# A two-layer hybrid encoder in split float32r products: operand start addresses moved to multiples of 256 bytes, and the head norm's weights applied at the transpose

## The chip, the cores and the metric

The kernel runs on one NeuronCore of one Trainium2 chip. The metric is the device time of one execution in microseconds, the median of several. Before the change that median is 2259.04 us, over three runs from 2258.91 to 2259.23 us.

## What is computed

An input of 256 tokens by 2048 features goes through two layers in float32. Layer 0 has one input projection whose columns feed a bidirectional matrix memory (four heads) and a bidirectional gated recurrence, and one output projection. Layer 1 has windowed attention with 16 heads. Each is followed by a gated feed-forward block, and every block begins with an RMS norm. The part of the reference that the change touches is the end of layer 0's mixer:

```python
hm = bidirectional_mlstm(qh, kh, vh, gates)
hm = hm * lax.rsqrt(jnp.mean(jnp.square(hm), axis=-1, keepdims=True) + RMS_EPS)
hm = jnp.transpose(hm, (0, 2, 1, 3)).reshape(B, S, MLSTM_WIDTH) * head_g.astype(jnp.float32)
y_a = hm * jax.nn.sigmoid(o.astype(jnp.float32))
...
y = jnp.concatenate([y_a, y_b], axis=-1).astype(h.dtype)
return y @ w_out
```

Here `head_g` has one weight for each of the 1024 features of `hm`.

## The kernel before

**Products.** Nearly all the work is the product of 256 tokens with about 400 MB of weights. To keep float32 accuracy each operand is split in two float32r parts, a high one (the value rounded to float32r) and a low one (what is left). The weights arrive through SP's DMA queue as tiles `raw` of 1 MB (four buffers). For each half of such a tile ScalarE casts the high part (`wh`, L204) and VectorE subtracts it to get the low part (`wl`, L205), three steps ahead of TensorE.

A matrix instruction has a **held** operand (128 columns, loaded into the array by a weight load that the trace shows on its own engine, PEld) and a **streamed** operand. There are two shapes of step:

- *Wide* steps (L294 and L295) hold 128 columns of weights and stream the activations. L294 holds the high weights and streams both parts of 256 tokens, 512 columns; L295 holds the low weights and streams the high part, 256 columns. All products whose outputs lie on partitions have this shape.
- *Narrow* steps (L272, L273, L274) hold 128 tokens of one part of the activations and stream 512 columns of weights: high by high, high by low, low by high.

Both parts together are 3712 pairs of wide and 3648 narrow instructions. The remaining matrix instructions are small: float32 ones (transposes at L141, the recurrence's gates at L454, the memory's scores at L681) and the attention's float32r ones (L861 to L863).

**Order.** The schedule is written out by hand. `emit_step` records the split of a later step, the products of this step, and then one stage of each background task; evacuations are generators that advance by one `yield` for each step. So the order of instructions on each engine is fixed when the program is built, and does not depend on times.

**Where tiles lie.** A pool allocates its tiles one behind the other in every partition, at byte addresses that follow from the sizes of all tiles allocated ahead of them. Tiles in pool `const` come first, in the order of their allocation (L130 to L138 and small ones later), then `raw`, `wh`, `wl`, 2 KB work tiles (`ev`), eight 8 KB slots (`slot`, of `SLOT` = 2064 floats) that hold activations such as `hT`, `ya`, `yb`, `oT`, `v`, five 4 KB tiles (`m4`, 1040 floats), and small ones. Start addresses in a partition, taken modulo 256, of the tiles that matrix instructions read:

```
tile                          before             after
cst (identity, triangles)     224                0
ehr                           224                0
ones                          32                 0
xT (activations, all wide)    96                 0
wh, wl (every buffer)         32                 0
ev tiles                      32                 0
8 KB slots 0..7               32 96 160 224 ...  0
4 KB tiles 0..4               32 96 160 224 32   0
```

The parts of these tiles that the products take begin at multiples of 512 bytes in them, so the offset of a tile is that of its operands. (In `v`, where a head is 1032 bytes, and for a few operands of 4 columns, this does not hold, before or after.) All starts before are odd multiples of 32 bytes.

**The head norm.** `o_chunk` (L780) makes the output gate: ScalarE writes tanh into an `ev` tile (L789), VectorE adds 1 and multiplies with `hgh`, a tile of 128 by 1024 that holds half of `head_g` on every partition (L794). GpSimd's queue loads it by a broadcast DMA (L999), VectorE halves it (L1002). `ml_out` (L744) multiplies the heads with their norm factors and this gate (L759), transposes the result on TensorE (L771), and splits the transpose into float32r parts (`ya`): a cast on ScalarE (L772) and a subtraction on VectorE (L773), each over two feature blocks at a time.

## Time and profile before

| What | Value |
|---|---|
| median of 3 runs | 2259.04 us |
| span of the profiled execution, first to last instruction | 2256.9 us |
| difference of the two (what lies around the span) | 2.1 us |
| TensorE busy with matrix instructions | 2240.3 us |
| TensorE weight loads | 1903.8 us |
| VectorE busy | 1391.3 us |
| ScalarE busy | 1097.7 us |
| GpSimd busy | 23.8 us |
| read from HBM | 414.09 MB, 184 GB/s over the span |

The busy time of an engine is the time in which at least one of its instructions runs. Matrix instructions overlap: the next starts while the one ahead is still on its way through the array. So a row of a matrix instruction gives a duration that is longer than the step from its start to the start of the next, and it is the step that adds up to the time.

### The profile page before, as it was taken

How to read it: one execution, taken by the hardware profiler on the slowest of the kernel's cores; microseconds unless marked ns; L12 is line 12 of the kernel's file. 1: busy time of each engine (PE TensorE's matmuls, PEld its weight loads, DVE VectorE, ACT ScalarE, POOL GpSimd, SP SyncE). 2: the span in 40 equal slices, each digit the busy share in tenths (PEclk: the TensorE clock that was granted, in tenths of full speed). 3: DMA queues.
4: the chain of work that ended last, by engine and by line, in shares of the span. 5: the costliest groups of instructions: out<-in, count | busy, mean ns of one | idle time of the engine just before them, and what ended most of it. 6: DMA issues, size and time to landing. Idle time of an engine off the chain costs nothing.

```text
span 2256.9 us, 29286 instructions
## 1 busy us (share of the span) xinstructions
PE 2240.3 (99%) x11660; PEld 1903.8 (84%) x11660; DVE 1391.3 (62%) x1960; ACT 1097.7 (49%) x1603; POOL 23.8 (1%) x42
## 2 busy tenths in 40 slices
PE   9999999999999999999999999999999999999998
PEld 7878888888888888888888888888888888888886
DVE  6867856666654466665566676556666544666654
ACT  5667545444443344444454554454444433444443
POOL 1000000000000000000000000000000000000000
PEclk9999999999999999999999999999999999999999
DMA  7534655555555555555555555445555555555553
GB/s 289 182 122 151 221 171 187 187 187 186 187 186 189 184 187 187 187 193 182 191 190 176 186 183 175 168 171 185 185 187 187 204 187 202 191 189 189 192 196 112
DMA packets 61354, 418.09 MB, mean 185 GB/s; under 512 B 6972, under 2 KB 7628, under 8 KB 12448
## 3 DMA queue, kind: packets, MB, share of 16 engines
q1 hardware_dynamic: 58176, 406.35, 52.1%
q0 software_dynamic: 2608, 9.26, 1.2%
q8 instruction: 91, 1.49, 0.3%
q10 hardware_dynamic: 432, 0.60, 0.1%
q14 instruction: 47, 0.39, 0.0%
HBM read 414.09 MB, written 2.10 MB: 184 GB/s over the span
## 4 chain that ended last, share of the span: by engine, by line
PE 95%; DVE 2%; ACT 1%; issue 1%; DMA 0%; SPq 0%; POOL 0%; POOLq 0%; DVEq 0%; ACTq 0%
PE acc L294 37%; PE acc L295 19%; PE acc L272 12%; PE acc L274 12%; PE acc L273 12%; DVE wl L205 1%; PE rgp L454 1%; ACT wh L204 1%; PE nT L141 0%; DVE xc L421 0%; DMA raw<-in_w_v 0%; PE apT L141 0%; PE num L724 0%; PE asc L862 0%; PE apo L861 0%
## 5 line engine op out<-in xcount | busy, mean ns | idle before, releaser
L205 DVE TENSOR_TENSOR wl<-raw,wh 128x1024 fp32r<-128x1024 f32 (+1 forms) x770 | 932.8, 1221 | 727.2 <-ACT wh L204 698.7
L294 PE MATMUL acc<-xT,wh 128*128 128x512 f32 x3712 | 1314.8, 396 | 0.4 <-ACT v L662 0.4
L204 ACT CAST wh<-raw 128x1024 fp32r<-128x1024 f32 (+1 forms) x770 | 802.0, 1044 | 568.3 <-PE acc L274 324.1
L295 PE MATMUL acc<-xT,wl 128*128 128x256 f32 x3712 | 1045.1, 282 | 0.0
L294 PEld LDWEIGHTS acc<-xT,wh 128*128 128x128 f32 x3712 | 697.8, 188 | 165.5 <-ACT v L662 0.6
L295 PEld LDWEIGHTS acc<-xT,wl 128*128 128x128 f32 x3712 | 696.8, 188 | 1.1 <-DVE wl L205 0.3
L272 PE MATMUL acc<-wh,hT 128*128 128x512 f32 x704 | 276.9, 393 | 0.0
L274 PE MATMUL acc<-wh,hT 128*128 128x512 f32 x704 | 275.9, 392 | 0.0
L273 PE MATMUL acc<-wl,hT 128*128 128x512 f32 x704 | 275.7, 392 | 0.0
L274 PEld LDWEIGHTS acc<-wh,hT 128*128 128x128 f32 x704 | 132.2, 188 | 29.9
L273 PEld LDWEIGHTS acc<-wl,hT 128*128 128x128 f32 x704 | 132.4, 188 | 29.0
L272 PEld LDWEIGHTS acc<-wh,hT 128*128 128x128 f32 x704 | 132.3, 188 | 28.8
L313 ACT CAST hT<-up 128x256 fp32r<-128x256 f32 x88 | 35.8, 406 | 198.7 <-DVE up L951 198.7
L934 ACT ACTIVATE up<-up 128x256 f32<-128x256 f32 x88 | 36.8, 418 | 157.8 <-DVE up L933 157.8
L272 PE MATMUL acc<-wh,xT 128*128 128x512 f32 x256 | 104.1, 407 | 0.5 <-ACT wh L204 0.5
L273 PE MATMUL acc<-wl,xT 128*128 128x512 f32 x256 | 101.3, 396 | 1.0 <-DVE wl L205 1.0
L274 PE MATMUL acc<-wh,xT 128*128 128x512 f32 x256 | 101.1, 395 | 0.0
L319 DVE TENSOR_TENSOR up<-acc,up 128x256 f32<-128x256 f32 x176 | 73.5, 418 | 1.5 <-ACT up L318 1.5
L318 ACT COPY up<-acc 128x256 f32<-128x256 f32 x176 | 64.2, 365 | 0.0
L314 DVE TENSOR_TENSOR hT<-up,hT 128x256 fp32r<-128x256 f32 x88 | 37.4, 426 | 41.6 <-ACT hT L313 41.6
L272 PEld LDWEIGHTS acc<-wh,xT 128*128 128x128 f32 x256 | 48.1, 188 | 12.5 <-ACT wh L204 1.5
L273 PEld LDWEIGHTS acc<-wl,xT 128*128 128x128 f32 x256 | 48.1, 188 | 11.8 <-DVE wl L205 1.6
(228 smaller groups left out, 1371.3 us busy)
## 6 DMA issues: line engine op xcount, KB each, us to landing
raw<-in_w SPq DMA_DIRECT2D x264, 1024.0 KB, 4.8
raw<-in_w_aqk SPq DMA_DIRECT2D x32, 1024.0 KB, 4.9
raw<-in_w_out SPq DMA_DIRECT2D x16, 1024.0 KB, 4.8
raw<-in_w_av SPq DMA_DIRECT2D x16, 1024.0 KB, 4.8
raw<-in_w_o SPq DMA_DIRECT2D x16, 1024.0 KB, 4.8
raw<-in_w_xr SPq DMA_DIRECT2D x8, 1024.0 KB, 8.6
raw<-in_w_qk SPq DMA_DIRECT2D x8, 1024.0 KB, 4.9
raw<-in_w_og SPq DMA_DIRECT2D x8, 1024.0 KB, 4.8
```

The source lines that it names most:

```text
L204: A.copy(hi[:, k], raw[:, k])
L205: V.tensor_tensor(lo[:, k], raw[:, k], hi[:, k].bitcast(F32), op=ALU.subtract)
L272: PE.matmul(acc, xh, hi[:, j, :], start=f, stop=False)
L273: PE.matmul(acc, xh, lo[:, j, :], start=False, stop=False)
L274: PE.matmul(acc, xl, hi[:, j, :], start=False, stop=e)
L294: PE.matmul(acc, wh[:, j, :], x2.rearrange("p a b -> p (a b)"), start=f, stop=False)
L295: PE.matmul(acc[:, :S], wl[:, j, :], x2[:, 0, :], start=False, stop=e)
L313: A.copy(dst[:, 0, :], src)
L314: V.tensor_tensor(dst[:, 1, :], src, dst[:, 0, :].bitcast(F32), op=ALU.subtract)
L318: A.copy(dst, acc[:, S:])
L319: V.tensor_tensor(dst, acc[:, :S], dst, op=ALU.add)
L934: A.activation(t, t, AF.Silu)
```

## The change

It does two things. Sizes and the order of allocation are changed so that the tiles of the products begin at multiples of 256 bytes: two tiles of 64 bytes go to the front, `cpk` is padded to 192 floats, a slot has 2112 floats in place of 2064, a 4 KB tile 1088 in place of 1040. And `hgh` shrinks from 1024 floats on every partition to 8: the weights lie by feature in `cpk` (columns 152 to 159), and are multiplied in where the transposed result is split, where a feature is a partition. The gate is then tanh + 1 alone, written in place. The DMA at L999 and the wait for step 16 go. Comments and docstrings are dropped as well, which moves line numbers.

```diff
-C_BA, C_BX, C_LAM = 104, 120, 136
-C_N = 152
+C_BA, C_BX, C_LAM, C_HG = 104, 120, 136, 152
+C_N = 160
...
-SLOT = 2064
+SLOT = 2112
...
-        t = m4p.tile([P, 1040], dt, tag="m4", name=name)
+        t = m4p.tile([P, 1088], dt, tag="m4", name=name)
...
-    cpk = const.tile([P, C_N], F32, name="cpk")
+    gbias = const.tile([P, 16], F32, name="gbias")
+    half = const.tile([P, 16], F32, name="half")
+    cpk = const.tile([P, 192], F32, name="cpk")[:, :C_N]
     cst = const.tile([P, 3, P], F32, name="cst")
     ehr = const.tile([MH, MH, P], F32R, name="ehr")
-    gbias = const.tile([P, 16], F32, name="gbias")
     ones = const.tile([P, P], F32, name="ones")
-    half = const.tile([P, 16], F32, name="half")
-    hgh = const.tile([P, 1024], F32, name="hgh")
     xT = const.tile([P, KB, 2, S], F32R, name="xT")
+    hgh = const.tile([P, 16], F32, name="hgh")[:, :RB]
...
-            A.copy(yt[:, 2 * p:2 * p + 2, 0, :], ps)
-            V.tensor_tensor(
-                yt[:, 2 * p:2 * p + 2, 1, :], ps, yt[:, 2 * p:2 * p + 2, 0, :].bitcast(F32), op=ALU.subtract
-            )
             for k in range(2):
+                kb = 2 * p + k
+                g = hgh[:, 4 * c + kb:4 * c + kb + 1]
+                A.mul(yt[:, kb, 0, :], ps[:, k, :], g)
+                V.scalar_tensor_tensor(
+                    yt[:, kb, 1, :], ps[:, k, :], g, yt[:, kb, 0, :].bitcast(F32), op0=ALU.mult, op1=ALU.subtract
+                )
                 flags.add(f"y{4 * c + 2 * p + k}")
...
-            es = []
+            go = ml["go"][:, :, c * CW:(c + 1) * CW]
             for t in range(2):
-                e = ev("oe")
-                A.activation(e, ch.acc[t], AF.Tanh, scale=ml["ro"][:, t:t + 1])
-                es.append(e)
+                A.activation(go[:, t, :], ch.acc[t], AF.Tanh, scale=ml["ro"][:, t:t + 1])
             ch.acc = None
             yield
-            for t in range(2):
-                V.scalar_tensor_tensor(
-                    ml["go"][:, t, c * CW:(c + 1) * CW], es[t], 1.0, hgh[:, c * CW:(c + 1) * CW],
-                    op0=ALU.add, op1=ALU.mult,
-                )
+            V.tensor_scalar(go, go, 1.0, None, op0=ALU.add)
...
-        while pos["split"] < 16:
-            yield
-        GP.dma_start(hgh, bcast(a["head_g"], 1024))
         while pos["split"] < 24:
             yield
-        V.tensor_scalar(hgh, hgh, 0.5, None, op0=ALU.mult)
+        V.tensor_scalar(hgh, cpk[:, C_HG:C_HG + RB], 0.5, None, op0=ALU.mult)
```

TensorE's instructions are the same ones in the same order before and after. On ScalarE and VectorE no row changes its place either, but rows change their form. The first two of the four transposed pieces of the matrix memory's result stand on ScalarE between the casts of weights (`wh<-raw`) like this before:

```order
197 L467 ACTIVATE rg_1749<-rg_1749 128x1024
198 L204 CAST wh<-raw 128x1024 x2
199 L772 CAST ya<-yT 128x2x256
200 L204 CAST wh<-raw 128x1024
201 L772 CAST ya<-yT 128x2x256
202 L204 CAST wh<-raw 128x1024
```

and like this after, where `hgh` is the column of weights:

```order
197 L468 ACTIVATE rg_1748<-rg_1748 128x1024
198 L205 CAST wh<-raw 128x1024 x2
199 L776 ACTIVATE ya<-yT,hgh 128x256 x2
200 L205 CAST wh<-raw 128x1024
201 L776 ACTIVATE ya<-yT,hgh 128x256 x2
202 L205 CAST wh<-raw 128x1024
```

One instruction of 512 elements has become two of 256 at the same place. On VectorE the same pieces stand before between the recurrence's work (`rgh`) and the weights' low parts (`wl`):

```order
249 L480 TENSOR_TENSOR rgh<-rgh,rg_1750 128x512
250 L773 TENSOR_TENSOR ya<-yT,ya 128x2x256
251 L205 TENSOR_TENSOR wl<-raw,wh 128x1024
252 L773 TENSOR_TENSOR ya<-yT,ya 128x2x256
253 L205 TENSOR_TENSOR wl<-raw,wh 128x1024
```

and after:

```order
249 L481 TENSOR_TENSOR rgh<-rgh,rg_1749 128x512
250 L777 SCALAR_TENSOR_TENSOR ya<-yT,hgh,ya 128x256 x2
251 L206 TENSOR_TENSOR wl<-raw,wh 128x1024
252 L777 SCALAR_TENSOR_TENSOR ya<-yT,hgh,ya 128x256 x2
253 L206 TENSOR_TENSOR wl<-raw,wh 128x1024
```

Here too one instruction has become two smaller ones, with the weights' column as a further operand, and nothing has moved past another row.

More of the change, by code (lines that the diff above doesn't have):

```diff
@@ L1167, in arrange @@
          per_partition(e_rg_ba[0].reshape(-1)), per_partition(e_rg_bx[0].reshape(-1)),
-         per_partition(e_rg_lam[0].reshape(-1))], axis=1)
+         per_partition(e_rg_lam[0].reshape(-1)), per_partition(e_head_g[0])], axis=1)
     rgw = np.stack([e_rg_wa[0], e_rg_wx[0]]).reshape(2, 2, RB // 2, 2, P, P)
@@ L1176, in arrange @@
         "gate_b": c(e_gate_b[0][perm]),
-        "head_g": c(e_head_g[0]),
         "cpk": c(cpk), "cst": cst, "ehot": ehot, "abias": ab,
```

## The prediction

> **What bounds the kernel now.** I read the page first: the span, the busy times, the granted clock, the chain that ended last, and the costliest groups.
>
> ```profile
> span 2256.9 us, 29286 instructions
> PE 2240.3 (99%) x11660; PEld 1903.8 (84%) x11660; DVE 1391.3 (62%) x1960; ACT 1097.7 (49%) x1603; POOL 23.8 (1%) x42
> ...
> PEclk9999999999999999999999999999999999999999
> ...
> PE 95%; DVE 2%; ACT 1%; issue 1%; DMA 0%; SPq 0%; POOL 0%; POOLq 0%; DVEq 0%; ACTq 0%
> ...
> L294 PE MATMUL acc<-xT,wh 128*128 128x512 f32 x3712 | 1314.8, 396 | 0.4 <-ACT v L662 0.4
> L295 PE MATMUL acc<-xT,wl 128*128 128x256 f32 x3712 | 1045.1, 282 | 0.0
> ...
> L272 PE MATMUL acc<-wh,hT 128*128 128x512 f32 x704 | 276.9, 393 | 0.0
> L274 PE MATMUL acc<-wh,hT 128*128 128x512 f32 x704 | 275.9, 392 | 0.0
> L273 PE MATMUL acc<-wl,hT 128*128 128x512 f32 x704 | 275.7, 392 | 0.0
> ```
>
> TensorE is busy for 99% of the span at its full granted clock and makes up 95% of the chain; the wide pairs (L294, L295) and the narrow instructions wait for almost nothing. So the time is a number of matrix instructions times the step from one start to the next, and no other engine counts unless TensorE gets faster.
>
> The step is not the duration in the row. I take it from the timeline, as the first and last row of regular runs: 14 wide pairs, then 15 narrow instructions, then 21 narrow ones a few microseconds later.
>
> ```profile
> 999.73 0.40 PE L294 MATMUL acc<-xT,wh 128*128 128x512 f32 x1
> ...
> 1004.68 0.39 PE L294 MATMUL acc<-xT,wh 128*128 128x512 f32 x1
> ...
> 1011.91 0.39 PE L272 MATMUL acc<-wh,hT 128*128 128x512 f32 x1
> ...
> 1015.31 0.39 PE L272 MATMUL acc<-wh,hT 128*128 128x512 f32 x1
> ...
> 1015.99 0.40 PE L272 MATMUL acc<-wh,hT 128*128 128x512 f32 x1
> ...
> 1020.89 0.39 PE L272 MATMUL acc<-wh,hT 128*128 128x512 f32 x1
> ```
>
> A wide pair takes (1004.68 - 999.73) / 14 = 353.6 ns. Its two rows say 396 + 282 = 678 ns, so each row is (678 - 353.6) / 2 = 162 ns longer than its step. I use that 162 ns throughout: an average narrow instruction steps by 393 - 162 = 231 ns.
>
> The two narrow runs are what this prediction rests on. They run the same line on the same shapes, both without a wait; the first steps by 3.40 us / 15 = 226.7 ns, the second by 4.90 us / 21 = 233.3 ns. What differs is the tile `hT`: by the program's allocation the first lies at 32 modulo 256, like the streamed weights, the second at 96. **So the step depends on start addresses.** Nothing in the trace of before lies at 0, since all large operands start at odd multiples of 32 bytes.
>
> **What the change is worth: the step.** How fast could the step be? The float32 products give one end. They run on the same array, and the program's list holds half as many of them as the trace, which records each twice:
>
> ```profile
> L454 PE MATMUL rgp<-xc,rgw 128*128 128x256 f32 x64 | 16.4, 379 | 0.0
> ...
> L141 PE MATMUL apT<-cst,asn 128*128 128x128 f32 x64 | 9.6, 272 | 0.0
> L862 PE MATMUL asc<-aqk 128*128 128x256 f32 x32 | 9.0, 282 | 0.0
> ...
> L863 PE MATMUL asc<-aqk 128*128 128x256 f32 x32 | 9.0, 281 | 0.0
> ```
>
> Less 162, a float32 record steps by 217 ns for 256 columns and by 110 ns for 128: 0.836 ns a column and 3 ns for each instruction. The float32r products that start in phase with each other (L862 and L863, both operands in one tile; and the first narrow run) step by 119 ns for 256 columns and 226.7 ns for 512, thus 0.421 ns a column, half of float32's price within 1%, and 11 to 13 ns for each instruction. So float32r streams twice as fast as float32, and pays some 9 ns more **at each instruction**, not for each column. [...]
>
> That gives two ends for aligned operands. The fast end: float32's 3 ns and half its column price, 512 x 0.418 + 3 = 217 ns and 256 x 0.418 + 3 = 110 ns. The slow end: the in-phase rows as they are, 226.7 and 119 ns, if only the phase between the operands matters and an offset of 32 bytes costs nothing. I take the fast end. A cost that comes once for each instruction, whatever its length, is what a start in the middle of a line would look like, and phase alone (231 to 226.7 ns) explains only 4 of the 14 ns that separate the average narrow step from the fast end.
>
> The sum, against the span of 2256.9 us:
> - wide pairs: 353.6 - (217 + 110) = 26.6 ns, times 3712 = 98.7 us;
> - narrow instructions: 231 - 217 = 14 ns, times 3648 = 51.1 us;
> - the attention's float32r products (192 like L862): 119 - 110 = 9 ns, 1.7 us;
> - float32 products: nothing, since their rows show no excess.
>
> That is 151.5 us less. At the slow end it is 353.6 - 345.7 = 7.9 ns x 3712 = 29.3, and 231 - 226.7 = 4.3 ns x 3648 = 15.7, together 45 us.
>
> The Trainium skill's page "TensorE: Matmul & The Clock Gate" (section "Wait — 56ns, not 53.3ns?") states that warm matmuls follow each other at N / 2.4 GHz and about 2.5 ns more, measured as 215.7 ns for 512 columns, and ties it to no address. By it the pair would take an estimated 325 ns and the gain would be some 162 us. The rows of before disagree with it by 11 to 18 ns.
>
> **What is given back.** Where TensorE already waits for others, a faster TensorE waits longer. The stages:
>
> ```profile
> 0.00:50.00 50.00, 47.04 (x221) 39.00 (x222) 31.67 (x49) 30.90 (x43) 6.73 (x14) 1.00 0.76 282
> ...
> 100.00:150.00 50.00, 47.04 (x219) 37.70 (x218) 35.08 (x61) 35.42 (x58) 1.06 (x2) 1.00 0.45 156
> 150.00:200.00 50.00, 48.38 (x235) 39.97 (x234) 37.27 (x66) 35.50 (x61) 0.00 (x0) 1.00 0.46 161
> ...
> 400.00:800.00 400.00, 400.00 (x2093) 341.31 (x2092) 233.79 (x294) 177.08 (x237) 0.00 (x0) 1.00 0.55 189
> ...
> 2200.00:2257.00 57.00, 48.78 (x213) 39.50 (x211) 27.67 (x34) 19.05 (x25) 1.13 (x2) 0.96 0.32 112
> ```
>
> (Columns: the stage and its length in us, busy time of PE, PEld, DVE, ACT, POOL with counts, clock, DMA share, GB/s.) From 400 to 800 us, as in the other long stages, TensorE has no gap; VectorE is busy for 58%, which becomes 63% at a 7% shorter stage, and the weights need 189 / 0.93 = 203 GB/s, where the first 50 us moved 282. So nothing else becomes the bound there. In the first 300 us it is different: TensorE waits 3.0 us at the start for data, and 3.0 and 1.6 us around the matrix memory's heads and the recurrence, on chains of ScalarE and VectorE whose length the change doesn't touch. These 300 us hold 300 / 2256.9 = 13% of the gain, 20 us; I take half of it as given back, 10 us, with 0 and 20 as ends. The last 8 us, where TensorE is done, stay.
>
> **The head norm.** The forms that come and go:
>
> ```profile
> L371 ACT ACTIVATE xT<-nT,cpk 128x256 fp32r<-128x256 f32 x8 | 3.8, 475 | 5.2 <-DVE xT L372 3.7 <-PE nT L141 1.5
> L372 DVE SCALAR_TENSOR_TENSOR xT<-nT,cpk,xT 128x256 fp32r<-128x256 f32 x7 | 3.4, 482 | 1.7 <-ACT xT L371 1.6
> ...
> L773 DVE TENSOR_TENSOR ya<-yT,ya 128x512 fp32r<-128x512 f32 x4 | 2.7, 687 | 1.9 <-ACT ya L772 1.9
> ...
> L794 DVE SCALAR_TENSOR_TENSOR go<-oe,hgh 128x512 f32<-128x512 f32 x4 | 2.6, 684 | 0.0
> ...
> L772 ACT CAST ya<-yT 128x512 fp32r<-128x512 f32 x4 | 2.3, 580 | 2.9 <-PE yT L141 2.9
> ...
> L1002 DVE TENSOR_SCALAR hgh<-hgh 128x1024 f32<-128x1024 f32 x1 | 0.7, 685 | 0.0
> ```
>
> On VectorE four pieces of 687 ns become eight like L372: 8 x 482 - 4 x 687 = +1.1 us. Four gates of 684 ns become two of 1024 elements, like L1002: 2 x 685 - 4 x 684 = -1.4 us; L1002 itself shrinks to 8 elements, at most -0.7 us. On ScalarE four casts of 580 ns become eight scalings like L371: 8 x 475 - 4 x 580 = +1.5 us. The broadcast of 512 KB goes. All this lies beside TensorE, covered by weights' products three steps ahead; without that cover it costs two chains of at most 0.4 us. I count nothing.
>
> **The sum.** 2256.9 - 151.5 + 10 = 2115.4 us of span, and 2.1 us around it (2259.04 less 2256.9): **2117.5 us**, 6.3% faster.
>
> **The rivals.**
> 1. *Phase alone.* Aligned operands are in phase, as in the first narrow run, and no more: 45 us less and 3 given back, 2217 us. For it: those are the only rows that exist of what is to come, and their cost of 11 to 13 ns may be float32r's own. Against it: the same for each instruction at 256 and 512 columns, where float32 pays 3.
> 2. *The step is float32r's own, or the offsets are fine already*: 2259 us, the head norm being hidden. Against it stand the two narrow runs, with 226.7 and 233.3 ns on nothing but another address. The Trainium skill's page "SBUF — State Buffer" (section "Door 1: The DMA port swizzle (why `[64,N]` ≈ `[32,N]`)", its note on cachelines) gives SBUF lines of 16 bytes, by which every start of before lies on a line already and this rival would hold; the two runs speak against it.
> 3. *Slower.* With every start at 0, the held operand of the next instruction and the stream of this one begin in the same bank at the same moment, and one waits once for the other: the price is the difference of the two narrow runs, 6.6 ns: on every narrow instruction over the run in phase, on every wide one over now. Narrow: 233.3 - 231 = 2.3 ns x 3648 = 8.4 us; wide: 2 x 6.6 ns x 3712 = 49.0 us; 2259 + 57 = 2316 us. It decides from a pair step of 353.6 + 1.2 = 354.8 ns on, which alone is 4.5 us. For it: nothing shows a start at 0. Against it: the run in phase is the fastest of all.
>
> **How the numbers follow.** The forecast, with any step between the two ends' middle and the fast end, has 0.66; phase alone 0.22; no change 0.05; slower 0.07. The range's low end is the fast end with nothing given back, and 1 ns of rounding on 11,000 steps: 2259 - 151.5 - 11 = 2096. The high end takes in rival 1 with its 3 us of rounding: 2220. The rest, 0.12 and some tails, is left out. A measurement of this kernel can tell about 0.2%, 4.5 us, from no change: faster 0.88, same 0.05, slower 0.07.
>
> **What would show it.** After, the rows L294 and L295 (of the old numbering) should read 379 and 272 in place of 396 and 282, and the narrow ones 379 for every tile alike; 389 and 281 would be rival 1. All `hT` tiles should step alike, in either case. TensorE's idle time from 0 to 300 us should grow by 10 us, and nowhere else by more than one. L773's successor should show eight pieces of about 480 ns and no longer wait in TensorE's chain. The prediction is wrong if the steps shrink but gaps open after 300 us, or if the steps of wide and narrow move in opposite directions.

## The result and the profile after

The changed kernel takes **2241.72 us** (median of four runs, 2241.69 to 2241.92) against 2258.97 us for the kernel before on the same chip: a ratio of 0.9923, with a 95% interval from 0.9909 to 0.9937. It is faster by 17 us. The prediction was 2117.5 us with a range from 2096 to 2220, so the direction was right and the time lies 22 us above the range.

The page of the changed kernel and its costliest matrix rows (its lines are one higher, so L295 and L296 are the wide pair, L273 to L275 the narrow instructions):

```profile
span 2239.9 us, 29291 instructions
PE 2221.5 (99%) x11660; PEld 1899.0 (85%) x11660; DVE 1390.2 (62%) x1962; ACT 1096.0 (49%) x1607; POOL 23.2 (1%) x41
...
L295 PE MATMUL acc<-xT,wh 128*128 128x512 f32 x3712 | 1307.7, 397 | 0.5 <-ACT v L663 0.5
L296 PE MATMUL acc<-xT,wl 128*128 128x256 f32 x3712 | 1040.8, 280 | 0.6 <-DVE wl L206 0.5
L273 PE MATMUL acc<-wh,hT 128*128 128x512 f32 x704 | 274.5, 390 | 0.0
L275 PE MATMUL acc<-wh,hT 128*128 128x512 f32 x704 | 274.0, 389 | 0.0
L274 PE MATMUL acc<-wl,hT 128*128 128x512 f32 x704 | 274.0, 389 | 0.0
...
```

TensorE is still what bounds the kernel: 99% busy, and the rows wait for almost nothing. The narrow rows fell from 392 or 393 to 389 or 390 ns. The wide rows read 397 and 280 where they read 396 and 282. The prediction had 379 and 272 for its forecast and 389 and 281 for its first rival; the narrow rows are the rival's, the wide pair is neither's as it stands.

The steps, from the timeline: first and last row of a run of wide pairs, and of a narrow run.

```profile
984.16 0.40 PE L295 MATMUL acc<-xT,wh 128*128 128x512 f32 x1
...
991.58 0.40 PE L295 MATMUL acc<-xT,wh 128*128 128x512 f32 x1
...
999.28 0.39 PE L273 MATMUL acc<-wh,hT 128*128 128x512 f32 x1
...
1009.48 0.39 PE L273 MATMUL acc<-wh,hT 128*128 128x512 f32 x1
```

A wide pair steps by 7.42 us / 21 = 353.3 ns, as much as in the stretch of before (353.6). A narrow instruction steps by 10.20 us / 45 = 226.7 ns, exactly the run "in phase" of before. So in a long run all narrow instructions now go at the best rate that the trace of before held.

For the wide pairs one stretch does not stand for all. Both traces have ten long runs of wide pairs (30 to 735 pairs each, 3037 of the 3712), and after its first few pairs each run keeps one pace to its end. The first instructions of pairs, counted over 200 us inside the four longest runs, in the changed kernel and then in the kernel before (columns: stretch and length in us, busy time of these instructions with their count, the same of their weight loads, clock, DMA share, GB/s):

```profile
400.00:600.00 200.00, 200.00 (x578) 107.88 (x577) 1.00 0.56 190
780.00:980.00 200.00, 200.00 (x567) 106.37 (x567) 1.00 0.55 187
1530.00:1730.00 200.00, 200.00 (x578) 107.89 (x577) 1.00 0.55 190
1910.00:2110.00 200.00, 200.00 (x567) 106.36 (x566) 1.00 0.55 188
```

```profile
400.00:600.00 200.00, 200.00 (x567) 106.35 (x566) 1.00 0.55 188
780.00:980.00 200.00, 200.00 (x568) 106.37 (x567) 1.00 0.55 189
1530.00:1730.00 200.00, 200.00 (x567) 106.37 (x567) 1.00 0.54 184
1930.00:2130.00 200.00, 200.00 (x575) 107.87 (x574) 1.00 0.55 188
```

From start to start these runs take 346.7, 353.3, 346.7 and 353.3 ns a pair after, and 353.3, 353.3, 353.3 and 348.8 ns before. Of all ten, four runs (1539 pairs) take 346.7 ns after and six (1498 pairs) 353.3; before, three (749 pairs) take 348.8 ns and seven (2288 pairs) 353.3. (200 us hold 577 pairs at 346.7 ns and 566 at 353.3; a row that reaches over an end of the stretch counts too.) So at one and the same set of starts a run of wide pairs takes one of two paces. The four executions of the changed kernel lie within 0.23 us of each other, and one run of 735 pairs at its other pace would add 735 x 6.6 ns = 4.9 us, so the paces hardly change from one execution to the next.

Means over the whole trace, worked out from all start times where TensorE did not wait, take in all runs and also the first instructions of each, which step differently:

| step, ns between starts | before | after | saved in all |
|---|---|---|---|
| narrow, `xT` held (768) | 233.2 | 228.3 | 3.8 us |
| narrow, other tiles held (2880) | 230.1 | 227.0 | 8.7 us |
| wide pair (3712) | 352.2 | 350.2 | 7.2 us |

Together 19.7 us. The wide pairs' share comes from the paces of the runs, not from a new step of every pair. TensorE's idle time grew from 2256.9 - 2240.3 = 16.6 us to 2239.9 - 2221.5 = 18.4 us, which gives 1.8 us back, and the span is 17.0 us shorter.

Where TensorE waits longer shows in the windows of the changed kernel (columns as in the prediction):

```profile
0.00:50.00 50.00, 46.80 (x220) 38.93 (x221) 31.27 (x49) 30.68 (x43) 6.21 (x13) 1.00 0.75 279
...
200.00:250.00 50.00, 48.22 (x234) 39.85 (x233) 35.08 (x64) 29.54 (x46) 1.05 (x1) 1.00 0.43 147
...
400.00:800.00 400.00, 400.00 (x2129) 345.23 (x2128) 237.83 (x300) 179.65 (x243) 0.00 (x0) 1.00 0.56 192
```

From 200 to 250 us the same view of before has

```profile
200.00:250.00 50.00, 49.97 (x240) 41.07 (x239) 36.99 (x65) 30.00 (x46) 1.05 (x1) 1.00 0.43 147
```

The idle time grew by 0.24 us in the first window, by 0.1 us each from 100 to 150 and from 150 to 200 us and by 1.75 us from 200 to 250 us, and it shrank by 0.33 us from 50 to 100 us: 1.9 us more in the first 300 us. It grew by nothing in the long stage from 400 us, where VectorE stands at 59% and HBM delivers 192 GB/s.

### The profile page after: what moved, and what is told of

It reads as the page before. It is cut to its first block, busy times and chain, and to the rows that moved or that the text cites. A ratio compares the mean times of both kernels' runs of the same rounds, so it can differ in the third digit from the quotient of the medians.

```text
span 2239.9 us, 29291 instructions
## 1 busy us (share of the span) xinstructions
PE 2221.5 (99%) x11660; PEld 1899.0 (85%) x11660; DVE 1390.2 (62%) x1962; ACT 1096.0 (49%) x1607; POOL 23.2 (1%) x41
## 4 chain that ended last, share of the span: by engine, by line
PE 95%; DVE 2%; ACT 2%; issue 1%; DMA 0%; SPq 0%; POOL 0%; POOLq 0%; DVEq 0%; ACTq 0%
PE acc L295 38%; PE acc L296 19%; PE acc L273 11%; PE acc L275 11%; PE acc L274 11%; ACT wh L205 1%; DVE wl L206 1%; PE rgp L455 1%; PE nT L142 0%; DMA raw<-in_w_v 0%; PE apT L142 0%; PE num L725 0%; DVE xres L346 0%; PE asc L860 0%; PE apo L860 0%
## 5 line engine op out<-in xcount | busy, mean ns | idle before, releaser
L295 PE MATMUL acc<-xT,wh 128*128 128x512 f32 x3712 | 1307.7, 397 | 0.5 <-ACT v L663 0.5
L296 PE MATMUL acc<-xT,wl 128*128 128x256 f32 x3712 | 1040.8, 280 | 0.6 <-DVE wl L206 0.5
L295 PEld LDWEIGHTS acc<-xT,wh 128*128 128x128 f32 x3712 | 696.2, 188 | 162.8 <-ACT v L663 0.6
L296 PEld LDWEIGHTS acc<-xT,wl 128*128 128x128 f32 x3712 | 701.3, 189 | 2.0 <-DVE wl L206 1.2
L273 PE MATMUL acc<-wh,hT 128*128 128x512 f32 x704 | 274.5, 390 | 0.0
L275 PE MATMUL acc<-wh,hT 128*128 128x512 f32 x704 | 274.0, 389 | 0.0
L274 PE MATMUL acc<-wl,hT 128*128 128x512 f32 x704 | 274.0, 389 | 0.0
L275 PEld LDWEIGHTS acc<-wh,hT 128*128 128x128 f32 x704 | 132.2, 188 | 27.4
L274 PEld LDWEIGHTS acc<-wl,hT 128*128 128x128 f32 x704 | 132.2, 188 | 27.3
L273 PEld LDWEIGHTS acc<-wh,hT 128*128 128x128 f32 x704 | 132.2, 188 | 27.3
L314 ACT CAST hT<-up 128x256 fp32r<-128x256 f32 x88 | 35.8, 406 | 198.6 <-DVE up L948 198.6
L273 PE MATMUL acc<-wh,xT 128*128 128x512 f32 x256 | 103.5, 404 | 0.7 <-ACT wh L205 0.6
L274 PE MATMUL acc<-wl,xT 128*128 128x512 f32 x256 | 100.2, 391 | 1.0 <-DVE wl L206 1.0
L275 PE MATMUL acc<-wh,xT 128*128 128x512 f32 x256 | 100.0, 390 | 0.0
L273 PEld LDWEIGHTS acc<-wh,xT 128*128 128x128 f32 x256 | 48.3, 189 | 12.0 <-ACT wh L205 1.5
L274 PEld LDWEIGHTS acc<-wl,xT 128*128 128x128 f32 x256 | 48.3, 189 | 10.6 <-DVE wl L206 1.6
```

What stands on the lines that cost most here:

```text
L273: PE.matmul(acc, xh, hi[:, j, :], start=f, stop=False)
L274: PE.matmul(acc, xh, lo[:, j, :], start=False, stop=False)
L275: PE.matmul(acc, xl, hi[:, j, :], start=False, stop=e)
L295: PE.matmul(acc, wh[:, j, :], x2.rearrange("p a b -> p (a b)"), start=f, stop=False)
L296: PE.matmul(acc[:, :S], wl[:, j, :], x2[:, 0, :], start=False, stop=e)
L314: A.copy(dst[:, 0, :], src)
```

## The experiments

Four theories were put to the test. **A:** the step of a float32r instruction depends on the distance, modulo 256 bytes, between the start of the operand held for the next instruction and the start of the operand streamed; a distance of zero is not free either. In the trace of before the load of L295's weights, 188 ns long, starts within 10 ns of the start of the L294 that streams meanwhile. **B:** the absolute start counts, as the prediction held. **C:** the gain comes from the head norm. **D:** other engines set the pace in the full kernel. "Phase" below is held start minus streamed start, modulo 256. Before, a wide step had phase 192 (32 - 96), a narrow one with `xT` held 64, the other narrow ones 0, 64, 128 or 192 by slot; after, all have 0.

### All starts 32 bytes further, phases kept

The changed kernel, with one small tile ahead of all others:

```diff
+    shift = const.tile([P, 8], F32, name="shift")
+    V.memset(shift, 0.0)
     gbias = const.tile([P, 16], F32, name="gbias")
```

> The changed kernel with one tile of 32 bytes put ahead of all others, so that every operand starts at 32 modulo 256 and the phase between held and streamed operands is as in the changed kernel. Theory A (the step depends on the phase between the operands alone, and float32r has a price of its own): narrow step 227 ns and wide pair 350 ns as in the changed kernel, 2242 us within 3. Theory B (what counts is a start on a multiple of 64 or 256 bytes): the gain goes, 2256 to 2260 us.

Measured: 2241.85 us, ratio 0.9923 (0.9909 to 0.9936), the time of the changed kernel. Its rows:

```profile
L297 PE MATMUL acc<-xT,wh 128*128 128x512 f32 x3712 | 1307.9, 397 | 0.5 <-ACT v L665 0.5
L298 PE MATMUL acc<-xT,wl 128*128 128x256 f32 x3712 | 1040.8, 280 | 0.7 <-DVE wl L208 0.7
L275 PE MATMUL acc<-wh,hT 128*128 128x512 f32 x704 | 274.5, 390 | 0.0
```

With every operand at 32 modulo 256 instead of 0 each duration is the same to the nanosecond. B falls: alignment as such is worth nothing here.

### The kernel before with slots in phase only

```diff
-SLOT = 2064
+SLOT = 2112
```

> The kernel before with slots of 2112 floats in place of 2064 and nothing else: the tiles hT, ya, yb, oT all lie at 32 modulo 256, as the weights' parts do; xT stays at 96. Theory A: narrow steps with these tiles fall from 230 to 227 ns (2880 of them, 8 to 9 us), narrow steps on xT stay at 233 and wide pairs at 352: 2250 us. Theory B (alignment to 0 counts): no change, 2259 us.

Measured: 2247.41 us, ratio 0.9948 (0.9936 to 0.996), 11.6 us faster, where A expected some 9. The narrow instructions with slots held fell from 230.1 to 227.0 ns, which gives 2880 x 3.1 = 8.9 us as expected; those with `xT` held stayed at 233.2. The other 3 us come from the wide pairs, whose mean fell from 352.2 to 351.4 ns although none of their starts moved: four of the ten long runs (1363 pairs) now took 348.8 ns, where three (749 pairs) had, and 614 x 4.5 ns = 2.8 us. So one number of the change gives two thirds of its gain, and which of its paces a run of pairs takes depends on more than its own starts.

### The kernel before with the new head norm only

The two edits of the head norm in the kernel before, `hgh` left at its size so that no start moves; its eight columns come by a small DMA of their own.

```diff
-            A.copy(yt[:, 2 * p:2 * p + 2, 0, :], ps)
...
+                A.mul(yt[:, kb, 0, :], ps[:, k, :], g)
...
-        GP.dma_start(hgh, bcast(a["head_g"], 1024))
+        GP.dma_start(hgh[:, :RB], a["head_g"])
```

> The kernel before with the head norm's weights applied at the transpose and every tile at the address it had (the weights come by a small DMA of their own in place of the broadcast). Theory A and B: no change beyond 0.1%, 2259 us, since these instructions lie beside TensorE. Theory C (the gain comes from the head norm): 2242 to 2250 us.

Measured: 2260.06 us, ratio 1.0004 (0.9996 to 1.0013). C falls. The edit is not quite free, though: TensorE, which was busy for 49.97 us from 200 to 250 us before, has a gap of 1.25 us here (the row of this run, then that of the kernel with slots in phase, which keeps the old head norm and is 11.6 us faster than before):

```profile
200.00:250.00 50.00, 48.75 (x232) 39.81 (x231) 34.84 (x62) 30.44 (x48) 1.05 (x1) 1.00 0.40 135
```

```profile
200.00:250.00 50.00, 49.97 (x242) 41.18 (x241) 36.98 (x66) 29.53 (x46) 1.05 (x1) 1.00 0.43 147
```

The matrix memory's products wait there for one instruction of VectorE (`w`, L710) for 1.2 us.

### TensorE alone, one shape at a time

A kernel that loads one block of the input and then runs 32 equal matrix instructions for each case (one execution, as for all the probes below), on tiles placed at chosen starts (`hd` held, `st` streamed):

```python
def run(h, s, n, times=32):
    for i in range(times):
        PE.matmul(o1[:, :n], h[:, i % 8 * P:i % 8 * P + P],
                  s[:, i % 2 * 512:i % 2 * 512 + n], start=True, stop=True)
for n in (512, 384, 256, 128):
    for h, s in ((0, 0), (32, 32), (0, 32), (32, 0), (64, 0), (128, 0), (192, 0)):
        run(hd[h], st[s], n)
```

> TensorE alone, everything else of the computation left out: runs of 32 matrix instructions that hold 128 columns and stream n columns, bfloat16 (n = 512, 256), then float32r with n = 512, 384, 256, 128 at start offsets of held and streamed operand 0/0, 32/32, 0/32, 32/0, 64/0, 128/0, 192/0 modulo 256. Theory A: bfloat16 steps by 216 ns at 512; float32r by 227 ns at 0/0 and at 32/32 alike, and by 229 to 234 at the other phases; the excess over bfloat16 at 0/0 grows with n if it is a price for each column (11 ns at 512, 5 at 256), and stays the same if it is one for each instruction. Theory B: 216 ns at 0/0, 227 at 32/32.

Four of its groups of 512 columns in the timeline (start, length of the group, count; `aligned` is a start at 0, `plusAA` at 32):

```profile
34.78 5.38 PE L58 MATMUL out<-staligned,hdaligned 128*128 128x512 f32 x23
...
41.84 5.38 PE L58 MATMUL out<-stplusAA,hdplusAA 128*128 128x512 f32 x23
...
48.67 5.99 PE L58 MATMUL out<-stplusAA,hdaligned 128*128 128x512 f32 x25
...
56.83 5.53 PE L58 MATMUL out<-staligned,hdplusAA 128*128 128x512 f32 x23
```

The step is the group's length less the last instruction's 0.39 us, over the count less one: (5.38 - 0.39) / 22 = 226.8 ns at 0 and 0, and the same at 32 and 32; 233.3 ns at the two mixtures (from all start times; the lines alone are good to 0.4 ns). Phases 64, 128 and 192 gave 233.2, 231.8 and 229.0 ns, and bf16 216 ns (215.8 at 512 columns and 109.2 at 256, so 106.6 / 256 = 0.417 ns, or 1 / 2.4 ns, a column). The Trainium skill's page "SBUF — State Buffer" (section "Door 1: The DMA port swizzle (why `[64,N]` ≈ `[32,N]`)") gives lines of 16 bytes; by these alone 0 and 32 would be alike in any mixture, and the mixtures are 6.5 ns slower. Two things follow. A holds for single instructions. And these five numbers yield the kernels' narrow steps: before, `xT` held has phase 64 (233.2 against 233.2 in the kernel); of the 22 tiles `hT`, 8 lie at phase 0, 7 at 192, 4 at 64 and 3 at 128 by the program's allocation, which gives 229.4 against 229.8 (the latter with the first instructions of each run); after, phase 0, 226.8 against 227.0. At 384 columns the step in phase was 173.3 ns, 13.3 over 384 / 2.4, as 226.7 is over 512 / 2.4.

### TensorE alone, wide pairs

The same with pairs as in L294 and L295 of before: 512 columns on the high part, then 256 on the low part, all streamed from a start at 0, with each of 16 combinations of starts for the two held tiles, and two more.

```python
for h in (0, 64, 128, 192):
    for l in (0, 64, 128, 192):
        pairs(st[0], hd[h], hd[l])
```

> TensorE alone, the rest of the computation left out: runs of 24 wide pairs (a stream of 512 columns on held high parts, then 256 of its columns on held low parts), with the stream at 0 and the high and low held parts each at 0, 64, 128, 192 modulo 256; then the phase of before (stream 64, held 32 and 32) and of the changed kernel moved by 32. Theory A (a float32r instruction costs n / 2.4 GHz and 13.3 ns, and phases between held and streamed operand add up to 10 ns): 347 ns a pair is the floor by single runs (226.7 + 120), no phase below 345; the phase of before near 352, that of the changed kernel near 350. Theory D (the pair's pace is set by other engines' accesses in the full kernel, not by phases): all phases alike here, near 347.

First and last rows of three combinations in the timeline (`plusBB` is a start at 64, `plusDD` at 192): both held at 0; high at 64 and low at 0; both at 192.

```profile
30.82 0.40 PE L63 MATMUL outw<-staligned,hdaligned 128*128 128x512 f32 x1
...
35.06 0.40 PE L63 MATMUL outw<-staligned,hdaligned 128*128 128x512 f32 x1
...
61.18 0.39 PE L63 MATMUL outw<-staligned,hdplusBB 128*128 128x512 f32 x1
...
68.32 0.39 PE L63 MATMUL outw<-staligned,hdplusBB 128*128 128x512 f32 x1
...
153.35 0.40 PE L63 MATMUL outw<-staligned,hdplusDD 128*128 128x512 f32 x1
...
160.42 0.39 PE L63 MATMUL outw<-staligned,hdplusDD 128*128 128x512 f32 x1
```

They hold 12, 21 and 20 pairs: 353.3, **340.0** and 353.5 ns. The phases of the two held tiles, high down and low across, in ns for a pair:

| | 0 | 64 | 128 | 192 |
|---|---|---|---|---|
| 0 | 353.3 | 346.7 | 346.7 | 350.0 |
| 64 | 340.0 | 353.3 | 350.0 | 353.3 |
| 128 | 351.7 | 346.7 | 351.1 | 346.7 |
| 192 | 340.0 | 346.7 | 346.7 | 353.3 |

This accounts for the runs at 353.3 ns of both kernels. Before, both phases were 192; after, both are 0; both cost 353.3 ns here. Even the sequence of steps is that of these runs: 237, 118, 231, 118, 233, 123 ns over three pairs at (192, 192) and, within 1 ns, in the kernel before; 236, 114, 232, 118, 240, 120 in the changed kernel, and at (0, 0) the same six lengths within 1 ns. The whole repeats every 1060 ns. The probe does not show the second pace of either kernel: each combination ran once, and one run shows one pace. A pair in which the 512 and the 256 columns both run at their best exists, 226.7 + 113.3 = 340.0 ns, but with the two weight tiles at different phases. The expectation had put the kernel before at another combination (stream 64, held 32: 346.7 ns); its phase is 192. And the combination at 32, 32, 32, which has the phases of (0, 0), settled at 346.7 ns, the second pace of the changed kernel: which repeating sequence a run falls into is not decided by phases alone. That pace is the sum of two single steps in phase, 226.7 + 120.0 ns. The floor of 345 ns that the expectation drew from such sums was missed by the two combinations at 340.0. As for D, the pairs' paces differ by 13 ns here, where no other engine runs beside them.

### TensorE alone, fewer held columns

Is the remaining price of 13.3 ns that of the weight load's length? The held operand was cut from 128 to 32 columns, other starts were meant to be tried, and the same operands were repeated.

```python
for m in (128, 96, 64, 32):
    cols(hd[0], st[0], m, 512)      # m held columns
for m in (64, 32):
    cols(hd[0], st[0], m, 256)
for o in (16, 96, 160, 224):
    run(hd[o], st[0], 512)
same(hd[0], st[0], 512)
```

> TensorE alone, the rest of the computation left out: float32r instructions that stream 512 columns at 0 and hold 128, 96, 64, 32 columns at 0; 256 columns with 64 and 32 held; held starts at 16, 96, 160, 224; one and the same pair of operands repeated; float32 with 256 columns. Theory A1 (the 13.3 ns come from the next instruction's weight load meeting the stream in the memory): fewer held columns take less, 227 ns at 128 columns held, about 223 at 64, 219 at 32. Theory A2 (they come from the start of the float32r stream itself): 227 ns whatever is held. Both: held starts other than 0 modulo 256 give 229 to 235; float32 216 ns.

Measured at 512 columns: 226.7, 230.0, 230.0 and 231.7 ns for 128, 96, 64 and 32 held columns; a shorter load makes it slower. At 256 columns it makes it faster: 113.3 ns with 64 and with 32 held columns, where 128 held columns took 120.0 in the first probe. So the price does depend on what is held, but does not fall with the load's length in general, as A1 of the expectation had it; A2, a step that is the same whatever is held, falls too. Repeating the same operands gave 226.7, and float32 with 256 columns 215.8 ns, where the prediction read 217 from the rows. The four other starts are void: the padding of 16 bytes was rounded up to 32 in the allocation, which moved all later tiles too, so that the cases named 16, 96, 160 and 224 lay at 32, 128, 192 and 0. They gave 233.3, 231.8, 229.0 and 226.7 ns, and so repeat the first probe's 233.3, 231.8, 229.0 and 226.8.

### The changed kernel with `xT` moved by 128 or 192 bytes

```diff
+    gap = const.tile([P, 32], F32, name="gap")
+    V.memset(gap, 0.0)
     xT = const.tile([P, KB, 2, S], F32R, name="xT")
+    gap2 = const.tile([P, 32], F32, name="gap2")
+    V.memset(gap2, 0.0)
```

(48 and 16 in place of 32 and 32 for 192 bytes.)

> The changed kernel with xT alone moved to 128 modulo 256, everything else at 0. Theory A: narrow steps with xT held go from 227 to 232 ns (768 of them, +4 us), those with other tiles stay at 227; wide pairs move by what the phase of 128 is worth, between 347 and 356 ns, so 2232 to 2268 us, and pairs and narrow steps may move in opposite directions. Theory B (alignment to 128 would do): 2242 us, no step changes.

> The changed kernel with xT alone moved to 192 modulo 256, everything else at 0. Theory A: narrow steps with xT held go from 227 to 229 to 233 ns (768 of them, +2 to +5 us), the others stay at 227; wide pairs between 347 and 356 ns, 2230 to 2268 us. Theory B: between 2242 and 2259 us with wide and narrow steps all slower.

Measured: 2246.9 us, ratio 0.9946 (0.9929 to 0.9963), and 2252.87 us, ratio 0.9973 (0.9963 to 0.9984). With `xT` at 128 the wide pairs have phases (128, 128) and stepped by 351.0 ns (probe 351.1); with it at 192 they have (64, 64) and stepped by 353.2 (probe 353.3). Narrow steps with `xT` held: 232.5 and 229.4 ns (probe 231.8 and 229.0). In both kernels all ten long runs keep the pace of the probe.

### TensorE alone, mixed starts and narrow triples

In the kernel one `wh` is held in wide steps and streamed in narrow ones, so a move of `wh` for the wide pairs changes the narrow phases. This probe took the remaining mixtures: pairs with odd offsets, and narrow triples as in L272 to L274 of before.

```python
for h, w in ((0, 0), (0, 64), (64, 64), (0, 192), (192, 192), (224, 192), (0, 32), (0, 224)):
    narrow(hd[h], st[w], st[0])     # activations held at h, wh at w, wl at 0
```

> TensorE alone, the rest of the computation left out. Wide pairs with the stream at 0, low held part at 0 and high held part at 32, 96, 160, 224 modulo 256, then low at 224 with high at 64 and 192; then narrow triples (stream high, low, high weights; held parts both at h) with low weights at 0 and h / high weights at 0/0, 0/64, 64/64, 0/192, 192/192, 224/192, 0/32, 0/224. Theory A (each instruction's excess is set by the phase of the operand that is loaded for the next one against the stream that runs meanwhile): triples take 3 x 226.7 = 680 ns at 0/0; at 0/64 two of three streams have the load at 192, 229 ns, so about 685; at 0/192 the load at 64, 233 ns, about 693; 192/192 has 0, 192, 0: about 682. Wide pairs between 340 and 353 ns.

Measured, for a triple: 680.0 ns with everything at 0 (3 x 226.7), 687 ns with activations and high weights both at 64, and 693 to 703 ns for all the others, more than the sums of single steps had let expect. No pair beat 340.0 ns; the best of the new ones took 344.4. Wide and narrow steps want different starts of the same tile.

### The changed kernel with `wh` moved by 64 or 192 bytes

```diff
+    gap1 = ctx.enter_context(tc.tile_pool(name="gap1", bufs=1)).tile([P, 48], F32, name="gap1")
     whp = ctx.enter_context(tc.tile_pool(name="whp", bufs=SPLIT_BUFS))
+    gap2 = ctx.enter_context(tc.tile_pool(name="gap2", bufs=1)).tile([P, 16], F32, name="gap2")
```

(For 192 bytes; 16 and 48 for 64.)

> The changed kernel with the high weight parts wh alone moved to 64 modulo 256, xT, wl and all else at 0. Theory A: wide pairs take the 340.0 ns that the probe showed for stream 0, high 64, low 0, against 350.2 now: 3712 x 10.2 = 38 us less; narrow steps rise from 227.3 to about 228.5, 4 us more: 2208 us, between 2203 and 2216. Theory B (alignment of all operands to 256 is best): slower than 2242 us. Theory D (other engines set the pace in the full kernel): 2242 us.

> The changed kernel with wh alone moved to 192 modulo 256. Theory A: wide pairs 340.0 ns again, 38 us less; narrow steps, whose load stands at 64 against two of three streams, rise towards 231 ns, 14 us more: about 2218 us. Theory B: slower than 2242 us. Theory D: 2242 us.

Measured: 2246.98 us, ratio 0.9947 (0.9934 to 0.9961), and 2230.75 us, ratio 0.9875 (0.9862 to 0.9889). Both missed the time expected, 2208 and 2218. The rows at 192:

```profile
L297 PE MATMUL acc<-xT,wh 128*128 128x512 f32 x3712 | 1271.4, 391 | 0.5 <-ACT v L665 0.5
L298 PE MATMUL acc<-xT,wl 128*128 128x256 f32 x3712 | 1025.3, 276 | 0.6 <-DVE wl L208 0.5
L276 PE MATMUL acc<-wl,hT 128*128 128x512 f32 x704 | 280.6, 399 | 0.0
L275 PE MATMUL acc<-wh,hT 128*128 128x512 f32 x704 | 280.4, 398 | 0.0
L277 PE MATMUL acc<-wh,hT 128*128 128x512 f32 x704 | 276.3, 393 | 0.0
```

At 192 the wide pair is at its best: 391 and 276 ns, and 340.3 ns between starts; the narrow rows rose to an average step of 234.3 ns. Against the changed kernel that is 3712 x (350.2 - 340.3) = 36.7 us won and 3648 x (234.3 - 227.3) = 25.5 us lost, 11.2 us in all; measured 11.0. The expectation had priced the narrow instructions from single steps; the probe's triples give them: 703.3 / 3 = 234.4 ns with `wh` at 192 and 700.0 / 3 = 233.3 at 64, against 234.3 and 233.3 in the kernels. At 64 the wide pair averaged 345.9 ns, since its runs have two paces again: only two of the ten long ones (1374 pairs) took the probe's 340.0 ns, and the other eight 350.0. The first instructions of its pairs, in one run of each:

```profile
400.00:600.00 200.00, 200.00 (x572) 107.30 (x572) 1.00 0.55 189
780.00:980.00 200.00, 200.00 (x590) 110.41 (x589) 1.00 0.57 196
```

So 16 us won on the pairs (3712 x 4.3 ns) stand against 22 us lost on the narrow triples (3648 x 5.9 ns). With `wh` at 192 all ten took 340.0.

### High weights at 192 in wide steps, at 0 in narrow ones

The changed kernel, with 64 more floats in each `wh` tile and a start that depends on the step's shape:

```diff
-        hi = whp.tile([P, 2, CW], F32R, tag="wh", name="wh")
+        o = 48 if st["wide"] else 0
+        hi = whp.tile([P, 2 * CW + 64], F32R, tag="wh", name="wh")[:, o:o + 2 * CW].rearrange("p (a b) -> p a b", a=2)
```

> The changed kernel with the high weight parts at 192 modulo 256 in wide steps only and at 0 in narrow steps, all else at 0: each kind of step gets the phases that were fastest for it. Theory A: wide pairs 340.3 ns (3712 x 9.9 = 37 us less than the changed kernel), narrow steps 227.3 as there: 2205 us, between 2202 and 2212. Theory B (alignment of all operands is best) and theory D (other engines set the pace): 2242 us.

Measured: **2205.9 us**, ratio 0.9765 (0.9751 to 0.9778), where 2205 was expected. It is faster than both kernels, by 53 and 36 us.

```profile
span 2204.1 us, 29291 instructions
PE 2184.9 (99%) x11660; PEld 1881.4 (85%) x11660; DVE 1388.9 (63%) x1962; ACT 1090.4 (49%) x1607; POOL 23.3 (1%) x41
...
L296 PE MATMUL acc<-xT,wh 128*128 128x512 f32 x3712 | 1271.5, 391 | 0.5 <-ACT v L664 0.5
L297 PE MATMUL acc<-xT,wl 128*128 128x256 f32 x3712 | 1025.5, 276 | 1.0 <-DVE wl L207 1.0
L274 PE MATMUL acc<-wh,hT 128*128 128x512 f32 x704 | 274.5, 390 | 0.0
L276 PE MATMUL acc<-wh,hT 128*128 128x512 f32 x704 | 274.0, 389 | 0.0
```

The wide rows are those of `wh` moved by 192, the narrow ones those of the changed kernel. The gain over the latter is 3712 x 9.9 ns = 36.7 us of steps, and 35.8 us were measured. D falls with it: at 53 us less than before no other engine has come to bound, and TensorE's idle time is 19.2 us.

### TensorE alone, lengths and steps of the stream

What is the price of 13.3 ns that stays in phase? Held and streamed tiles at 0, other lengths, and then 512 columns that all read one element (step 0) or every second one (step 2).

```python
for n in (512, 448, 320, 288, 256, 192):
    one(lambda i, n: st[0][:, i % 2 * 512:i % 2 * 512 + n], n)
one(lambda i, n: st[0][:, i % 2 * 512:i % 2 * 512 + 1].to_broadcast([P, 512]), 512)
one(lambda i, n: st[0][:, :].rearrange("p (a b) -> p a b", b=2)[:, :, 0], 512)
```

> TensorE alone, the rest of the computation left out: float32r, held and streamed operand at 0, stream of 512, 448, 320, 288, 256, 192 columns; then 512 columns that are all one and the same element (step 0), then 512 columns at a step of two elements. Theory P (a pause of 6.7 ns for each 256 columns or part of them, so that 512 and 384 cost the same 13.3 ns more than n / 2.4 GHz): 200, 146.7, 133.3 ns for 448, 320, 288, and 113.3 or 120 for 256. Theory Q (one start price of 13.3 ns for each instruction): the same for 448, 320 and 288, but 120 for 256. Theory R (a price for each column, 1/16): 198, 141.7, 127.5 ns. If the price is that of moving from line to line in the memory, it is gone with step 0 (216 ns); if it is that of the float32r format, it stays at 226.7.

Groups in the timeline: bf16, float32r at step 1, step 0 and step 2, each of 512 columns.

```profile
20.12 4.05 PE L58 MATMUL out<-stbf,hdbf 128*128 128x512 bf16 x18
...
31.67 5.61 PE L72 MATMUL out<-staligned,hdaligned 128*128 128x512 f32 x24
...
60.83 6.42 PE L72 MATMUL out<-staligned,hdaligned 128*128 128x512 f32 x29
...
69.77 12.41 PE L72 MATMUL out<-staligned,hdaligned 128*128 128x512 f32 x27
```

With the last instruction's length taken off (0.38, 0.39, 0.38 and about 0.61 us) the steps are 216, 227, **216** and about 453 ns. A float32r stream that stays on one element runs like bf16, and one that covers twice the memory takes twice as long. So the price is not that of the format alone: it needs a stream that moves on through memory. Whether step 2 is slow for the memory it covers or for its step was not tried apart. The other lengths, 448, 320, 288 and 256, gave 202.5, 146.7, 131.7 and 120.0 ns, that is 16, 13, 12 and 13 ns over n / 2.4: nearly one price for each instruction, though none of the three readings in the expectation fits every length. 192 columns took 111.7 ns, as 128 did, so there the stream's length no longer sets the step; that the weight load of 128 columns, the same in both, sets it is likely, but not shown.

## Why the prediction was wrong

- **The step that failed is "I take the fast end".** The forecast gave aligned operands 217 and 110 ns. The price it meant to remove is real: narrow instructions in phase pay 13.3 ns over 512 / 2.4, and the prediction's 11 to 13 ns for each instruction, whatever its length, was read rightly from the rows. But it took this for "a start in the middle of a line", and no row stood behind that. Starts at 0 and at 32 give the same 226.8 ns, and moving the whole changed kernel by 32 bytes changes no row. Of the 151.5 us forecast, alignment gives none.
- **The float32 rows were a poor end.** That float32 pays 3 ns and float32r 13 was taken as a sign that the 13 can be had. The same array does reach 216 ns, but only for bf16 or for a float32r stream that stays on one element. The Trainium skill's page "TensorE: Matmul & The Clock Gate" (section "Wait — 56ns, not 53.3ns?") with its 215.7 ns for 512 columns agrees with the bf16 group (216 ns), and no float32r stream over memory here reached it.
- **The narrow half of the first rival was right.** Its 226.7 ns is the step measured, and its 15.7 us for these instructions compare with 12.5 (the means include the start of each run, which is slower, above all after wide steps).
- **The wide half of the first rival was only half right, and this is why the time lies outside the range.** It took a pair in phase for the sum of two single steps in phase, 226.7 + 119 = 345.7 ns, and 7.9 ns x 3712 = 29.3 us. Long runs at that pace exist (346.7 ns), but they are half: the others take 353.3 ns at the same starts, precisely what most runs took before. The means differ by 2.0 ns, 7.2 us, and 22 of the rival's 45 us are missing. The runs that stay at 353.3 hold the mean 3.5 ns over 346.7, which makes 13 us; the kernel before averaged 352.2 and not the 353.6 of the stretch that was read, 5 us; and 346.7 in place of 345.7 is 4 us. The bound of the range, 2220 us, fell with them. That 353.6 was not the pace of all pairs could be seen in the trace of before, whose last long run takes 348.8 ns; a pair at another phase was not in it, so the lower end should have been zero for the wide pairs.
- **The price of 119 ns for 256 columns in phase** was right for a run of its own kind (120.0 in the probe), but it is the slowest of the phases there, not the fastest: at other phases 256 columns took 116.8 to 118.6 ns, and 113.3 in the best pairs and with fewer held columns. "In phase is the fastest of all", said against the third rival, holds for 512 columns, not for 256.
- **The attention's 1.7 us** did not come; its rows read 281 to 283 ns after, 280 to 282 before. The operands of the scores (`aqk`) lay in one tile, hence in phase, already.
- **Given back:** 10 us were set against a gain of 151.5, half of the 13% that fall into the first 300 us. Of a gain of 17, half of 13% would be 1.1 us; the first 300 us show 1.9 and the whole span 1.8. The place was right, the reason was not: the idle time was to grow because TensorE got faster, but 1.2 of the 1.75 us from 200 to 250 us come with the new head norm at the old addresses, and the kernel with slots in phase got 11.6 us faster with no gap there. In the changed kernel the matrix memory's products wait for ScalarE and VectorE for 6.0 us in place of 4.6, 1.2 of them for `w`, as with the head norm alone (5.8):

```profile
L725 PE MATMUL num<-v,w 128*128 128x257 f32 x48 | 13.5, 391 | 6.0 <-ACT hacc L735 2.3 <-DVE w L698 1.6 <-DVE w L711 1.2
```

- **The head norm is nearly hidden:** 1.0004 (0.9996 to 1.0013) by itself, where nothing was counted; its 1.1 us (2260.06 against 2258.97) lie within the interval, but a gap of 1.2 us is in the trace. The prediction's sign that its pieces are not in TensorE's chain failed: two pieces of L777 stand in the chain that ended last, 0.41 us each, and no such piece did before. The changed kernel has its pieces as forecast, eight of 471 and 482 ns, and two gates of 688:

```profile
L777 DVE SCALAR_TENSOR_TENSOR ya<-yT,hgh,ya 128x256 fp32r<-128x256 f32 x8 | 3.9, 482 | 3.7 <-ACT ya L776 3.7
L776 ACT ACTIVATE ya<-yT,hgh 128x256 fp32r<-128x256 f32 x8 | 3.8, 471 | 10.6 <-DVE ya L777 8.4 <-PE yT L142 2.2
...
L794 DVE TENSOR_SCALAR go<-go 128x1024 f32<-128x1024 f32 x2 | 1.4, 688 | 0.0
```

- **What bounds the kernel** was read rightly, apart from this gap: where a sum of steps was set beside a run above, the time followed it to within 1 us.
- **The third rival** (a collision at equal starts) had the right place in the wide pairs, where equal starts are indeed not the best, but not its size: it asked for a pair above 354.8 ns, and the slower pace is 353.3.

## What to carry to other kernels

Read the step from start to start, and where it differs between runs of one line and shape, place the operands and measure: 32 instructions for each start modulo 256 in a kernel of their own gave here the narrow steps of a kernel of 11,000 instructions within 1 ns. Measure the sequence that the kernel runs, pairs or triples, since single steps did not add up; and a tile that plays two parts may need two starts. Take the pace of every long run, not of one stretch: here runs of the same instructions at the same starts kept two paces, 2% apart, over hundreds of pairs. And try the best starts in the kernel itself: two combinations showed 340.0 ns for a pair in the probe, and only one of them kept it in every long run. A trace that shows only one state of a resource bounds nothing about the others: where the best rate seen is already in it, forecast that rate and keep "no gain" as the lower end for the shapes that it does not show.

## What the runs showed of the hardware

- A float32r instruction of 512 columns stepped by 226.7 to 233.3 ns, in runs of equal instructions, by the starts of its operands modulo 256; bf16 by 216 ns.
- The price needs a stream that moves through memory: at step 0 it is gone (216 ns), at step 2 the step doubles (about 453 ns). Fewer held columns made 512 columns slower (231.7 ns for 32) and 256 columns faster (113.3 ns for 64 or 32, 120.0 for 128).
- Wide pairs fall into repeating sequences and keep them for as long as a run lasts, up to 735 pairs. At one set of starts a run took one of two paces: 353.3 or 346.7 ns at phases (0, 0), 353.3 or 348.8 at (192, 192), 340.0 or 350.0 at (64, 0). At (192, 0) all runs took 340.0. Slots moved elsewhere changed the choice with no wide operand moved.

Open stays what in the memory or in TensorE's reading makes the phase matter and what the 13.3 ns are; and what decides which of its paces a run of pairs takes, where the two kernels with all starts at 0 and all at 32 agree in the eight longest runs and differ in the two shortest. The runs show where these prices lie, not their cause.
